# Layer 0's S5 tables and scan on VectorE, a gate's modulation on TensorE, and a reordered opening

## The chip, the cores and the metric

One core of a Trainium2 chip runs the whole program in one launch. The metric is the device time of an execution in microseconds; three runs of the kernel before gave a median of 1206.25 us.

## The reference

Two layers of a hybrid backbone work on 256 context tokens and 256 latent tokens of width 1024. Cut to what matters here (per layer, `p` its weights):

```python
sh1, sc1, ga1, sh2, sc2, ga2 = split(silu(c) @ w_mod[l] + b_mod[l], 6)     # and the same with c_ctx
h = rms_norm(x, g_norm1) * (1 + sc1) + sh1
z = h @ w_in[l]                    # 5 blocks of 256 for the mixers, then 4 gates of 1024
s5: bu = B_bar u;  states = associative_scan(a, bu) forward and backward (complex, 16 groups x 64)
    y = C_re h_re - C_im h_im + d * u;  y = gelu(y);  y = y * sigmoid(y @ w_glu)
fnet: real(fft2(u)) @ w;  pool: centred means of 2, 4, 8, 16, minus u
conv: v * sigmoid(gate), 31 taps, layer norm, silu, @ w
x = x + ga1 * (sum_k sigmoid(gate_k) * (branch_k @ w_branch_k)) @ w_out
x = x + ga2 * (relu(h2 @ w1) ** 2) @ w2          # h2: modulated with sh2, sc2
```

The context passes through layer 0 in full and through layer 1 only as far as the S5 states, which the latent scans inherit. Before the first layer a positional embedding is added to the latent tokens; behind the last stands an RMS norm.

## The kernel before

All tokens lie transposed: 128 features on the partitions, 512 token columns (context 0 to 255, latent 256 to 511) free, `X` in eight such tiles. Each large product is done on TensorE as three fp32r matmuls of a split operand (`mm3`): weight tiles arrive by DMA into three raw buffers, ScalarE copies the high part (`Stream.high`), VectorE subtracts to get the remainder (`Stream.low`, 1024 elements), and a tile of 128 outputs takes 24 matmuls (`tile_mm`). Both kinds of parts are in the tile "parts". The weight stream's DMAs go on SP's queue in the order of `plan`.

The order of instructions on each engine is the order of emission, which a planner makes in Python. TensorE's large products are emitted in a fixed order (`layer`, `order`). Between them, `pump` steps through background generators (`start(gen, classes, rank)`): the lowest rank that is ready goes first, provided that the modelled clock of each engine in its classes is at most a lead (2 us for VectorE and ScalarE, 5 for GpSimd) ahead of TensorE's modelled clock. A generator's `yield "w", t` makes it ready t modelled us later. Each engine executes its own list in order and waits on semaphores. The modelled clocks come from `Engines`: a cost per instruction, without waits between engines. `finish` emits all of a task that is left, and stands ahead of each branch's use (`y` in the order string: pool, FNet, convolution, S5).

The S5 branch of layer 0 needs tables from its parameters. `prep` makes the discretised `bbar` and the powers `base` on VectorE (some thirty short stretches of 16-element operations), and `rev`, the powers reversed, with nine copies on GpSimd. `tables_b` makes eight units: six products and sums of 256 elements each on VectorE, four TensorE transposes, a ScalarE copy and a store to DRAM (`scr_b`). `tables_c` makes eight units likewise on GpSimd (classes "pa"), with small matmuls and stores to `scr_c` and `scr_k`, its C loaded in pieces on SP's queue. In layer 0 both have two buffers (`nb = 2`), and the products of a unit are emitted after the next unit's elementwise work. Then `S5L.run` loads tables and u back (`load_u`, on GpSimd's queue), `states` makes the local states on TensorE, and `scan` runs a three-level up-sweep, seven small steps and a three-level down-sweep: the forward direction on GpSimd, the backward one on VectorE, five operations per level each (`level`). `readout` follows. Both scan tiles and the convolution's buffers of layer 0 carry the tile name "scan". The convolution is 62 `scalar_tensor_tensor` steps of 512 elements on VectorE with rank 4. For layer 1 the same table functions run on GpSimd beside layer 0's MLP, in one buffer (`nb = 1`), with waits of 8.0 and 2.0 around each unit's products; the tile is named "tables".

Modulation: the first shift and scale of layer 0 (`w_mod`, sixteen parts of 512 KB) are made on TensorE in the opening (`mod_part`, eight matmuls each; `mod_finish`). All others, from the first gate `ga1` (tiles 16 to 23) on, are made by `mods` on VectorE: per tile of 128 outputs a load (`w_modt`) and two accumulating operations of 1024 elements, rank 7.5, started after FNet's branch is used.

The opening (`run`, and the first branch of `layer`): x, modulation and first weight tiles are loaded; the position is added on VectorE and, for tiles 1, 3 and 5, on GpSimd; ScalarE squares; VectorE adds the eight squares up; TensorE sums over partitions; the norm's chain follows (`norm_steps`), then `h_tiles` makes the split input tile by tile, while `group(k, j)` emits the three matmuls of contraction tile k for output tile j and `parts` the modulation parts. `warm` emits matmuls whose result is not used.

## Time and profile before

| | before |
|---|---|
| three runs, us | 1206.25 median, 1205.58 to 1209.96 |
| the profiled execution, us | 1209.18 |
| its span, first to last instruction, us | 1207.2 |
| mean granted TensorE clock | 0.986 |
| TensorE, VectorE, ScalarE, GpSimd busy, us | 1160.9, 976.1, 517.1, 282.9 |

PE is TensorE's matmuls, PEld its weight loads, DVE VectorE, ACT ScalarE, POOL GpSimd, SP the queue of SyncE. Nearly all instructions carry the line of one helper (L64), so tiles tell them apart. Matmul rows of fp32 count two per instruction. An engine's idle time costs nothing unless another waits for it; the granted clock is given as a share of 2.4 GHz. Each fall of the clock in this trace lasts 3.4 or 6.8 us at 0.5.

### The profile page before, as it was taken

How to read it: one execution, taken by the hardware profiler on the slowest of the kernel's cores; microseconds unless marked ns; L12 is line 12 of the kernel's file. 1: busy time of each engine (PE TensorE's matmuls, PEld its weight loads, DVE VectorE, ACT ScalarE, POOL GpSimd, SP SyncE). 2: the span in 40 equal slices, each digit the busy share in tenths (PEclk: the TensorE clock that was granted, in tenths of full speed). 3: DMA queues.
4: the chain of work that ended last, by engine and by line, in shares of the span. 5: the costliest groups of instructions: out<-in, count | busy, mean ns of one | idle time of the engine just before them, and what ended most of it. 6: DMA issues, size and time to landing. Idle time of an engine off the chain costs nothing.

```text
span 1207.2 us, 20297 instructions
## 1 busy us (share of the span) xinstructions
PE 1160.9 (96%) x7770; PEld 1009.4 (84%) x7770; DVE 976.1 (81%) x1878; ACT 517.1 (43%) x872; POOL 282.9 (23%) x319
## 2 busy tenths in 40 slices
PE   7999897999999999999999899999899999999997
PEld 5777675777888988888887778898899999999997
DVE  6789989977999769999988883546998788867764
ACT  4534242344324365422332333346544556645543
POOL 0038656000000100166555561020520001000000
PEclk9999999999999999999999999999899999999999
DMA  9543531644674514466578774425554545555551
GB/s 366 225 144 109 180 92 52 229 156 138 212 229 156 173 37 148 140 188 230 186 245 296 249 247 180 130 98 177 173 166 167 159 160 205 177 190 179 189 182 48
DMA packets 66513, 211.49 MB, mean 175 GB/s; under 512 B 7984, under 2 KB 13616, under 8 KB 66416
## 3 DMA queue, kind: packets, MB, share of 16 engines
q1 hardware_dynamic: 55456, 183.84, 45.4%
q10 hardware_dynamic: 7696, 14.56, 3.3%
q0 software_dynamic: 3264, 11.80, 2.9%
q8 instruction: 61, 1.00, 0.3%
q14 instruction: 36, 0.29, 0.1%
HBM read 199.19 MB, written 10.98 MB: 174 GB/s over the span
## 4 chain that ended last, share of the span: by engine, by line
PE 72%; DVE 15%; POOL 3%; DMA 3%; issue 3%; ACT 3%; ACTq 0%; POOLq 0%; DVEq 0%; SPq 0%
PE bank L64 72%; DVE scan L64 5%; DVE parts L64 4%; DVE mixer L64 2%; DVE whole L64 2%; ACT parts L64 2%; POOL tables L64 1%; POOL whole L64 1%; ACT whole L64 1%; DVE windows L64 1%; POOL scan L64 1%; DMA whole<-in_w_in_dram 1%; DMA whole<-in_x_dram 0%; DMA scan<-scr_z 0%; DMA scr_c<-tables 0%
## 5 line engine op out<-in xcount | busy, mean ns | idle before, releaser
L64 PE MATMUL bank<-parts 128*128 128x512 f32 (+2 forms) x4008 | 727.2, 339 | 19.0 <-DVE parts L64 16.6
L64 PEld LDWEIGHTS bank<-parts 128*128 128x128 f32 x4008 | 616.3, 191 | 105.4 <-DVE parts L64 22.3
L64 ACT ACTIVATE parts<-whole 128x1024 fp32r<-128x1024 f32 (+1 forms) x288 | 273.7, 959 | 144.9 <-PE bank L64 73.9
L64 DVE TENSOR_TENSOR parts<-whole,parts 128x1024 fp32r<-128x1024 f32 (+1 forms) x240 | 294.0, 1233 | 16.0 <-ACT parts L64 15.6
L64 PE MATMUL bank<-hidden,parts 128*128 128x256 f32 (+1 forms) x1440 | 251.2, 335 | 0.0
L64 PEld LDWEIGHTS bank<-hidden,parts 128*128 128x128 f32 x1440 | 217.5, 188 | 29.9 <-issue 0.3
L64 DVE SCALAR_TENSOR_TENSOR whole<-whole 128x1024 f32<-128x1024 f32 (+4 forms) x188 | 175.7, 936 | 15.2 <-DMA whole<-in_w_modt_dram 12.0
L64 POOL TENSOR_TENSOR whole<-whole 128x256 f32<-128x256 f32 (+1 forms) x69 | 50.3, 743 | 347.2 <-ACT whole L64 342.2
L64 DVE SCALAR_TENSOR_TENSOR whole<-bank,whole 128x256 f32<-128x256 f32 (+1 forms) x121 | 54.7, 475 | 66.4 <-PE bank L64 66.2
L64 ACT ACTIVATE whole<-whole 128x256 f32<-128x256 f32 (+2 forms) x139 | 48.9, 388 | 107.2 <-DVE whole L64 96.4
L64 ACT ACTIVATE mixer<-bank 128x512 f32<-128x512 f32 (+1 forms) x84 | 40.7, 496 | 119.8 <-PE bank L64 110.3
L64 DVE TENSOR_TENSOR whole<-whole 128x256 f32<-128x256 f32 (+7 forms) x158 | 73.0, 467 | 16.7 <-ACT whole L64 11.7
L64 ACT ACTIVATE whole<-bank 128x512 f32<-128x512 f32 (+2 forms) x69 | 35.5, 537 | 109.1 <-PE bank L64 77.5
L64 POOL TENSOR_TENSOR tables<-tables,whole 128x256 f32<-128x256 f32 x48 | 61.4, 1287 | 37.4 <-DMA scr_c<-tables 34.9
L64 DVE TENSOR_TENSOR hidden<-whole,hidden 128x512 fp32r<-128x512 f32 (+2 forms) x77 | 53.4, 698 | 9.0 <-ACT hidden L64 2.4
L64 ACT ACTIVATE hidden<-whole 128x512 fp32r<-128x512 f32 (+2 forms) x77 | 47.1, 615 | 8.2 <-PE bank L64 2.3
L64 ACT ACTIVATE tables<-bank 128x512 f32<-128x512 f32 (+2 forms) x20 | 8.4, 422 | 92.8 <-PE bank L64 92.5
L64 POOL COPY whole<-whole 128x32 f32<-128x32 f32 x20 | 11.9, 626 | 150.3 <-DVE whole L64 150.3
L64 POOL TENSOR_TENSOR scan<-scan,whole 128x256 f32<-128x256 f32 (+3 forms) x50 | 44.0, 892 | 12.0 <-DVE scan L64 8.3
L64 DVE SCALAR_TENSOR_TENSOR scan<-scan,whole 128x512 f32<-128x512 f32 (+1 forms) x64 | 42.7, 728 | 0.0
L64 PE MATMUL bank<-merged,parts 128*128 128x256 f32 (+1 forms) x240 | 38.0, 316 | 0.8 <-DVE merged L64 0.8
L64 DVE TENSOR_TENSOR scan<-scan,whole 128x256 f32<-128x256 f32 (+5 forms) x61 | 31.5, 543 | 9.0 <-ACT whole L64 8.0
(115 smaller groups left out, 899.0 us busy)
## 6 DMA issues: line engine op xcount, KB each, us to landing
whole<-in_w_dram SPq DMA_DIRECT2D x128, 512.0 KB, 4.3
whole<-in_w_in_dram SPq DMA_DIRECT2D x84, 512.0 KB, 4.3
whole<-in_w_modt_dram SPq DMA_DIRECT2D x78, 512.0 KB, 4.1
whole<-in_w_br_dram SPq DMA_DIRECT2D x16, 512.0 KB, 4.4
whole<-in_w_out_dram SPq DMA_DIRECT2D x16, 512.0 KB, 4.2
mixer<-in_w_mod_dram SPq DMA_DIRECT2D x8, 512.0 KB, 9.7
scan<-scr_b POOLq DMA_DIRECT2D x8, 512.0 KB, 5.2
scan<-in_w_mod_dram SPq DMA_DIRECT2D x6, 512.0 KB, 9.7
```

The lines of the kernel that those rows point to most:

```text
L64: return f(out, *a, **k)
```

## The change

- Cost model: 0.14 + 1.055e-3 per element on VectorE; an fp32r matmul of n columns counts n + 32 in place of n; lags 2.75 and 1.71 in place of 2.5 and 1.52.
- Two kinds of background wait are new: `"u", e, t` (ready t after the later of TensorE's and engine e's modelled clocks) and `"at", t` (ready at a modelled time). They replace fixed waits in the tables of layer 0, pool, convolution and S5's end.
- `tables_b` and `tables_c` (both layers): five small ScalarE copies lay out the operands, and `turned` does a unit in three operations of 512 elements. Layer 0's `tables_c` and `scan_tables` run on VectorE; layer 1's stay on GpSimd, with one C buffer instead of two and 2.0 more wait after every second unit. ScalarE negates C.
- Scan (both layers): the backward direction's states are stored reversed (by ScalarE), so that one operation of up to 1024 elements does both directions, all on VectorE, four per level. `readout` reverses them back with two ScalarE copies per group.
- Modulation tiles 16 to 23 are made by `mods_pe` on TensorE (eight parts, from a new layout `w_modg`), a task that starts with the convolution and is finished ahead of FNet's use; `mods` starts at tile 24.
- Opening: position in one load at the head of ScalarE's queue, the parameters of S5 ahead of x on SP's queue; three early warm-up matmuls instead of seven; all position adds on VectorE; squares are added in pairs and TensorE sums each pair into one bank (`self.sums`); `prep` steps, parts and groups are interleaved more finely; ten modulation loads ahead of the norm instead of eight.

```diff
-                n = (n if a[1].dtype == F32R else 4 * max(n, 96)) * min(1.0, out.shape[0] / 128)
+                n = n + 32 if a[1].dtype == F32R else 4 * max(n, 112) * min(1.0, out.shape[0] / 128)
...
+    def turned(self, E, out, x, y, P, space):
+        sh, t = [128, 4, 16, 8], self.K.tmp()
+        w = []
+        for i, p in enumerate(P):
+            w.append(space[:, 32 * i:32 * i + 32])
+            self.K.nc.scalar.activation(w[i].rearrange("p (r q s) -> p r q s", r=2, q=2),
+                                        bc(p[:, None], [128, 2, 2, 8]), AF.Copy)
...
+        E.tensor_tensor(ov, bc(x[:, :, :, None], sh), wv[0], op=MUL)
+        E.tensor_tensor(tv, bc(y[:, :, :, None], sh), wv[1], op=MUL)
+        E.tensor_tensor(out, out, t, op=ADD)
...
     def tables_b(self, A, E):
-            E.tensor_tensor(ba[:, 0], Bb[0], Pb[0], op=MUL)
-            E.tensor_tensor(tmp, Bb[1], Pb[1], op=MUL)
-            E.tensor_tensor(ba[:, 0], ba[:, 0], tmp, op=SUB)
-            E.tensor_tensor(ba[:, 1], Bb[0], Pb[1], op=MUL)
-            E.tensor_tensor(tmp, Bb[1], Pb[0], op=MUL)
-            E.tensor_tensor(ba[:, 1], ba[:, 1], tmp, op=ADD)
+            nc.scalar.activation(x, bb[:, :, k, qs], AF.Copy)
+            nc.scalar.activation(y[:, 0], bb[:, 1, k, qs], AF.Copy, scale=-1.0)
+            nc.scalar.activation(y[:, 1], bb[:, 0, k, qs], AF.Copy)
+            self.turned(E, BAs[i % nb], ..., P, space[:, 128:192])
             yield
             if nb == 1:
                 yield "w", 8.0
+            done.append(nc.clock["d"])
             if i >= nb - 1:
+                yield "at", done[i + 1 - nb] + 0.5
                 products(i + 1 - nb)
...
+    def level(self, i, p0, step, n, g0=0):
+        x, cur = at(p0 - 2 ** i), at(p0)
+        E.tensor_tensor(t1, x, w(self.WR[i]), op=MUL)
+        E.tensor_tensor(t2, x[:, ::-1], w(self.WI[i]), op=MUL)
+        yield
         E.tensor_tensor(cur, cur, t1, op=ADD)
-        E.tensor_tensor(t2[:, h:2 * h], at(p0 - d, 0, 16), w(self.WI[i][k], 16, 32), op=MUL)
         E.tensor_tensor(cur, cur, t2, op=ADD)
...
+    def mods_pe(self):
+        for g in range(2):
+            for kp in range(4):
+                nc.sync.dma_start(raw, self.I["w_modg"][g][kp])
+                yield "w", 7.0
+                for k in range(2):
+                    for j in range(4):
+                        nc.tensor.matmul(bank[32 * j:32 * j + 32, 0:128], self.CACT[:, 2 * kp + k, :], w[:, k, j],
+                                         start=kp == 0 and k == 0, stop=kp == 3 and k == 1, tile_position=(0, 32 * j))
+                yield "w", 1.0
...
     def run(self):
-            self.tab0.append(self.start(self.pre[0].tables_c(half[1], nc.gpsimd), "pa", 2.5))
+            self.tab0.append(self.start(self.pre[0].tables_c(half[1], nc.vector), "da", 2.5))
             self.tab0.append(self.start(self.pre[0].tables_b(half[0], nc.vector), "d", 3.5))
...
-            (nc.gpsimd if k in (1, 3, 5) else nc.vector).tensor_tensor(x, x, pe, op=ADD)
+            nc.vector.tensor_tensor(x, x, pe, op=ADD)
...
+            if k % 2:
+                nc.vector.tensor_tensor(sq[k - 1], sq[k - 1], sq[k], op=ADD)
+                for i in range(4):
+                    nc.tensor.matmul(self.sums[:, i:i + 1], sq[k - 1][:, 128 * i:128 * i + 128], self.ones[:, 0:1],
+                                     start=k == 1 and i == 0, stop=k == 7 and i == 3)
+                if k < 5:
+                    self.warm(1)
```

## Rows read from the trace of the kernel before

**Rows 1.** page, part 1: busy time, share of the span, instructions

```profile
PE 1160.9 (96%) x7770; PEld 1009.4 (84%) x7770; DVE 976.1 (81%) x1878; ACT 517.1 (43%) x872; POOL 282.9 (23%) x319
```

**Rows 2.** windows by stage: stretch, length, busy PE PEld DVE ACT POOL, PEclk, DMA, GB/s

```profile
22.50:54.50 32.00, 30.84 (x293) 22.74 (x294) 22.85 (x70) 17.06 (x30) 0.00 (x0) 1.00 0.65 260
76.00:215.00 139.00, 123.32 (x722) 96.04 (x721) 130.54 (x223) 48.85 (x122) 94.05 (x114) 0.94 0.33 110
215.00:420.00 205.00, 205.00 (x1248) 167.22 (x1247) 176.85 (x292) 76.58 (x107) 6.10 (x7) 1.00 0.56 187
640.00:740.00 100.00, 95.79 (x502) 75.87 (x502) 78.38 (x109) 35.50 (x81) 55.92 (x63) 0.98 0.75 257
855.00:920.00 65.00, 60.33 (x580) 57.77 (x580) 63.84 (x149) 28.66 (x46) 23.85 (x31) 0.95 0.44 147
```

**Rows 3.** waits of PE, 76 to 215 us: total us, times, longest

```profile
PE bank L64 <- DVE parts L64: 7.8, 1, 7.8
PE bank L64 <- POOL scan L64: 3.9, 2, 2.1
PE bank L64 <- DMA scan<-scr_z: 2.2, 1, 2.2
PE bank L64 <- DVE scan L64: 1.6, 2, 1.0
```

**Rows 4.** busy us in a short stretch at the largest wait, columns as in rows 2

```profile
208.00:216.00 8.00, 4.58 (x12) 3.64 (x13) 7.96 (x11) 1.06 (x1) 3.01 (x4) 0.57 0.40 143
```

**Rows 5.** groups by form, 76 to 215 us: busy us, mean ns | idle before

```profile
L64 DVE TENSOR_TENSOR scan<-whole 128x256 f32<-128x256 f32 x16 | 12.5, 782 | 0.0
L64 DVE TENSOR_TENSOR scan<-scan 128x512 f32<-128x512 f32 x4 | 6.0, 1495 | 0.1
L64 DVE SCALAR_TENSOR_TENSOR scan<-scan,whole 128x512 f32<-128x512 f32 x44 | 29.7, 740 | 0.0
L64 POOL TENSOR_TENSOR scan<-scan,whole 128x256 f32<-128x256 f32 x38 | 32.9, 875 | 1.9 <-DMA scr_c<-scan 0.4
L64 POOL TENSOR_TENSOR scan<-scan,whole 128x512 f32<-128x512 f32 x2 | 6.2, 3120 | 1.8 <-issue 1.7
L64 ACT ACTIVATE scan<-whole 64x64 f32<-64x64 f32 x16 | 4.1, 255 | 5.3 <-POOL scan L64 5.1
```

**Rows 6.** groups by form on DVE, 1000 to 1180 us, GpSimd silent

```profile
L64 DVE TENSOR_TENSOR hidden<-whole,hidden 128x256 fp32r<-128x256 f32 x32 | 13.6, 425 | 3.3
```

**Rows 7.** groups by form on DVE, 340 to 420 us

```profile
L64 DVE SCALAR_TENSOR_TENSOR whole<-whole 128x1024 f32<-128x1024 f32 x9 | 11.0, 1223 | 0.2
L64 DVE TENSOR_TENSOR mixer<-mixer 128x512 f32<-128x512 f32 x9 | 6.2, 691 | 0.3
```

**Rows 8.** timeline of the opening: start us, us, engine, operation, count

```profile
4.47 6.32 PE L64 MATMUL bank<-whole 128*128 128x256 f32 x14 [4.47 <-DMA whole<-in_x_dram]
13.38 3.26 PE L64 MATMUL bank<-whole 128*128 128x256 f32 x16
15.71 0.16 DVE L64 TENSOR_SCALAR whole<-bank 128x4 f32<-128x4 f32 x1 [1.15 <-PE bank L64]
20.68 0.68 DVE L64 TENSOR_TENSOR whole<-whole,bank 128x512 f32<-128x512 f32 x1
```

**Rows 9.** groups by form on PE, 0 to 55 us: modulation parts

```profile
L64 PE MATMUL bank<-mixer,whole 128*32 128x128 f32 x128 | 4.7, 276 | 0.5 <-DMA mixer<-in_w_mod_dram 0.5
```

**Rows 10.** the tile scr_c, 76 to 215 us: its DMAs

```profile
DMA to landing us min/median/max: 2.0/2.1/5.1
```

**Rows 11.** waits of PE, 640 to 740 us

```profile
PE bank L64 <- POOL tables L64: 4.2, 3, 3.0
```

**Rows 12.** groups by form on POOL, 500 to 740 us

```profile
L64 POOL TENSOR_TENSOR tables<-tables,whole 128x256 f32<-128x256 f32 x48 | 61.4, 1287 | 37.4 <-DMA scr_c<-tables 34.9
```

**Rows 13.** waits of PE, 855 to 920 us

```profile
PE bank L64 <- DVE parts L64: 4.6, 2, 3.2
```

More of the change, by code (lines that the diff above doesn't have):

```diff
@@ L273, in tables_b @@
         nb = 2 if l == 0 else 1
-        BAs, BATs = [A(512) for _ in range(nb)], [A(512) for _ in range(nb)]
+        BAs, BATs, spaces = [[A(w) for _ in range(nb)] for w in (512, 512, 192)]
         def products(i):
@@ L324, in load @@
         def load(u):
-            (nc.gpsimd if l else nc.sync).dma_start(CCs[u % 2], K.I["s5c"][l][u])
-        load(0)
-        load(1)
+            (nc.gpsimd if l else nc.sync).dma_start(CCs[u % nb], K.I["s5c"][l][u])
+        for u in range(nb):
+            load(u)
         yield "w", 2.6
@@ L571, in scan @@
[L571 to L582 removed]
+        self.ST = [T(1024), T(1024)]
@@ new lines, in scan @@
+        S = self.SB.rearrange("p (a g n) -> p a g n", a=32, g=2)
+        E.memset(S[:, :, 0, 0:1], 0.0)
+        C3 = C.rearrange("p (a n) -> p a n", n=9)
+        Cr = C.rearrange("p (r a n) -> p r a n", r=2, n=9)
+        E.memset(C3[:, :, 0:1], 0.0)
+        for i, p0, step, n in ((0, 1, 2, 16), (1, 3, 4, 8), (2, 7, 8, 4)):
+            yield from self.level(i, p0, step, n)
+        C4 = C3[:, :, 1:9].rearrange("p a (g n) -> p a g n", g=2)
+        E.tensor_copy(C4, S[:, :, :, 8:33:8])
+        t1, t2 = [t[:, 0:32].rearrange("p (r a) -> p r a", r=2) for t in self.ST]
@@ L629, in readout @@
                 yield from K.hold(2)
+                back = K.tmp()[:, 0:256].rearrange("p (r q n) -> p r q n", r=2, q=4)
+                for r in range(2):
+                    nc.scalar.activation(back[:, r], SB[:, r, 1, 4 * h:4 * h + 4, g, 0:32][:, :, ::-1], AF.Copy)
+                yield "u", "a", 0.5
+                yield from K.hold(2)
                 py = [K.aux(), K.aux()]
@@ L925, in said @@
                 task["cls"] = y[1]
+            elif y[0] == "u":
+                c = self.nc.clock
+                task["ready"] = max(c["t"], c[y[1]]) + y[2]
+            elif y[0] == "at":
+                task["ready"] = y[1]
             else:
@@ L1059, in mods @@
                 yield
-        for i in range(16, 96):
+        for i in range(24, 96):
             l, m = i // 48, i % 48
@@ L1309, in weight @@
                 gw.append(self.stream.take(("in", l, gm[j])))
+            prep = tab[0]
             parts(2)
-            self.warm(2)
-            norm = self.norm_steps(((self.ACC,),), 512, 1024)
+            norm = self.norm_steps((), 512, 1024, pss=[self.sums])
             next(norm)
@@ L1346, in layer @@
             next(h)
-            group(1, 1)
+            self.step(prep, 1)
+            group(2, 0, 1)
+            parts(1)
+            weight(2)
+            group(3, 0, 1)
+            parts(1)
+            self.step(prep, 3)
             group(0, 2)
             group(1, 2)
-            self.step(tab[0], 3)
-            group(2, 0, 1, 2)
             parts(1)
+            group(2, 2)
             weight(3)
-            group(3, 0)
             parts(1)
-            group(3, 1)
-            parts(1)
-            parts(1)
-            group(3, 2)
             self.mod_finish(4)
@@ L1438, in layer @@
         tconv = self.start(br.conv(), "d", 4.0)
+        if l == 0:
+            tgate = self.start(self.mods_pe(), "a", 3.2)
         tasks = {2: task, 3: tconv}
@@ L1697, in make0 @@
             yield from self.pre[0].prep(half[1])
-            self.tab0.append(self.start(self.pre[0].tables_c(half[1], nc.gpsimd), "pa", 2.5))
+            self.tab0.append(self.start(self.pre[0].tables_c(half[1], nc.vector), "da", 2.5))
             self.tab0.append(self.start(self.pre[0].tables_b(half[0], nc.vector), "d", 3.5))
         self.tab0.append(self.start(make0(), "d", 0.0))
-        self.mod_load()
-        while self.stream.load():
-            pass
-        self.step(self.tab0[0], 1)
-        self.mod_ahead = 8
+        prep = self.tab0[0]
+        self.step(prep, 1)
+        for k in range(0, 8, 2):
+            nc.sync.dma_start(self.X[:, k:k + 2, :], I["x"][:, k:k + 2, :])
+        for ahead in (3, 4, 8):
+            self.mod_ahead = ahead
+            self.mod_load()
+            self.stream.load()
+            if ahead == 4:
+                self.step(prep, 1)
+        self.mod_ahead = 10
         self.mod_load()
         nc.vector.memset(self.CACT, 0.0)
-        self.warm(7)
+        self.step(prep, 2)
         t = self.tmp()
```

284 lines of the change are left out of this document (137 added, 147 removed).

## The prediction

> **What bounds the kernel now.** I read the page's busy shares first, then busy time and granted clock by stage, then what TensorE waited for in the stages where it was not full, and then what the other engines' instructions cost there. TensorE is busy for 96% of the span, VectorE for 81%, GpSimd for 23% [rows 1]. So the gain of any edit is limited to the places where TensorE does not run, or runs at its lower clock. By stage [rows 2] TensorE is full at clock 1.00 from 215 to 420 us: nothing that this change does to VectorE can shorten that. The poor stages are 76 to 215 us (layer 0's mixer while its S5 tables and scan are made: TensorE 123.3 of 139 us, clock 0.94, VectorE 130.5, GpSimd 94.1), 640 to 740 us (layer 1's tables: clock 0.98) and 855 to 920 us (layer 1's scan: clock 0.95).
>
> In the first of these TensorE waits 15.5 us: 7.8 for one weight remainder (parts) that stands on VectorE behind the scan, 3.9 for table products on GpSimd, 2.2 for the stored u (scr_z), whose load stands on GpSimd's queue behind its small table operations, 1.6 for table products on VectorE [rows 3]. The clock of 0.94 takes another 0.06 x 139 = 8.3 us; every fall stands behind one of these waits. In the last one TensorE works only 4.6 of 8 us while the clock is 0.57 [rows 4]; I take 1.4 us of the loss as lying inside the wait, so 6.9. Together 22.4 us are to be had here.
>
> Why VectorE and GpSimd run late shows in the durations. While both work, a VectorE product of 256 elements takes 0.78 us, GpSimd's 0.88, and the scan's VectorE additions of 512 take 1.50 [rows 5]; with GpSimd silent a 256 product takes 0.43 [rows 6], and 512 take 0.69 [rows 7]. The emitter's cost model (0.12 + 1.04e-3 per element) prices them as alone, so it issues work on which TensorE then waits.
>
> The Trainium skill (SBUF — State Buffer, "SBUF: two separate sides") says that VectorE with two SBUF inputs and GpSimd take one port pair by an exclusive lock, so that the loser waits for the other's whole instruction. 0.43 becoming 0.78 agrees. By the rule the convolution's operations, which read two SBUF inputs too, should also be shortened by the change; their row says 0.740 us beside GpSimd [rows 5], which leaves little to gain, and I count nothing for them.
>
> **The change part by part.**
>
> *Tables and scan of layer 0.* Before, 48 products of 256 on VectorE (at 0.78: 37 us) and 48 on GpSimd (at 0.88: 42 us); after, 16 units of three operations of 512 on VectorE, 48 x 0.69 = 33 us, none on GpSimd. The merged scan has six levels of four operations; by 0.69 for 512 elements, 1.22 for 1024 [rows 7] and 0.43 for 256 it is 8 x (1.22 + 0.69 + 0.43) = 18.7 us on VectorE, where before both engines shared it at 1.50 and 3.12 for one 512 operation [rows 5]. So VectorE's load stays near 130 us, and what exceeds the stage is the convolution's 44 steps (rank 4, at 0.74), which may slide into 215 to 420 us, where VectorE has 205 - 176.9 = 28 us free [rows 2]. The cross-engine order goes (no GpSimd result is waited for, u's load is free at once), and the model's costs (0.14 + 1.055e-3: 0.68 for 512) become what the rows show. All 15.5 + 6.9 could go.
>
> What is late next: each unit on VectorE waits for five small ScalarE copies (0.255 us each [rows 5]: 1.3 us); a CA buffer is used again two units later, after its store has landed (2.1 us median, 5.1 at most [rows 10]); and ScalarE negates C itself, hence waits for that load. VectorE is in order, so its weight remainders stand behind such a wait. Bounds: 0, when the two-deep buffers cover it, and 16 x 1.3 = 21 us, when every copy group is waited for in full and TensorE with it. The products come one unit late, which covers most; I take 4 us.
>
> *First gate's modulation on TensorE.* 16 accumulations of 1.22 us [rows 7] (19.5 us) leave VectorE in a stretch where TensorE does not wait for it: nothing gained. TensorE gets eight parts, now in a full stage: 128 rows, which are eight parts, took 4.7 us [rows 9]. Bounds 0 (they fall into gaps) and 4.7 plus a late load; I take 4.7. So the stage is -22.4 + 4 + 4.7 = -13.7 us.
>
> *Opening.* The norm's chain begins at 15.7 us and the first layer-0 tile input at 20.7 [rows 8]. Before, the last square is followed by up to five adds of 0.69 in a row; after, by one, as TensorE sums pairs. That is 2 to 2.8 us, less what the three position adds that come from GpSimd cost (3 x 0.43 = 1.3, partly while x arrives). From 22.5 to 54.5 us TensorE is busy 30.8 of 32 us [rows 2], so spreading the groups finds about 1 us. Against this, the table preparation's steps, its two loads (one now ahead of x on SP's queue) and the steps' small operations are moved into this stretch on VectorE. Bounds -6 and +3; I take -2.5.
>
> *Layer 1's tables stay on GpSimd*, with three operations of 512 for six of 256. TensorE waited 4.2 us for them [rows 11], with 0.02 x 100 = 2 us of clock [rows 2]. A unit was 6 x 1.29 = 7.7 us of work after a wait for the store of 34.9 / 7 = 5.0 us [rows 12]: 12.7 us, and the slot must be about 12.5, since three of sixteen were late. The waits in modelled time become 6% shorter in real time (a matmul of 512 columns counted 512, now 544): a slot of 11.9. No row shows a GpSimd product of 512 beside this work: at least 1.29 (a 256 one), at most 3.12 [rows 5]. I take 1.29 + 0.88 = 2.1, one more 256's length on top: 3 x 2.1 + 5.0 = 11.3, on time. I take -3 of the 6.2 us.
>
> *Layer 1's scan* goes to VectorE whole. VectorE is full there (63.8 of 65 us), TensorE waits 4.6 us for weight remainders [rows 13] and loses 0.05 x 65 = 3.3 to the clock [rows 2]. The work that comes over costs about what the slowing took; but two ScalarE permutations ahead of the wait are not touched. Bounds 0 and -7.9; I take -4. The remaining waits ("u" and "at" for fixed ones, longer lags) sit on tasks that run beside full TensorE stages: 0, within 3 either way.
>
> Sum: -2.5 - 13.7 - 3 - 4 = -23.2 us. The profiled execution took 1209.18 us (span 1207.2 and 2.0 around it), so 1186.0; it was 2.9 above the median of the runs, 1206.25, on which scale the forecast is 1183 us.
>
> **Rivals.**
>
> *The waits come back in another form* (half the gain): VectorE stands behind ScalarE's copies and the stores, so that of layer 0's stage 12 us more stay, and opening and layer 1's scan give 3 less: 1183 + 15 = 1198. For it: VectorE has only 8 us free in the stage and every weight remainder passes it. Against: TensorE's largest wait is one event behind contended operations.
>
> *A cold opening.* The early warm-up matmuls fall from seven to three. At the start fourteen rows of 256 columns took 6.32 us, 0.45 each, which is the lower level, 1.2 GHz; later sixteen rows, half of them sums of one column, took 3.26 [rows 8]. If the rise comes only with the dense groups, parts, warm-ups and the first groups double: some 6 us more, partly while data is awaited: opening +3, total 1189. The Trainium skill (TensorE: Matmul & The Clock Gate, "What's actually happening") holds that the throttled state is the default and activity releases it, which speaks for this rival; the rise in the trace after the unbroken warm-ups agrees.
>
> *The other side: layer 1's tables on GpSimd become the bound.* If an operation of 512 takes 3.12 us there, as one did in the scan, a unit of tables_c is 3 x 3.12 + 5.0 = 14.4 against 11.9, 2.5 us late eight times, and one of tables_b, which starts 2.0 + 1.3 us after the last products, 12.7, 0.8 late: 26 us, and after each of the eight long waits a clock fall of 1.7 us, as after the one long wait now: 40 us. With the other gains of 20 it gives 1206 + 20 = 1226. It decides from 2.6 us per operation on (8 x 0.9 + 13.6 = 21). For it: the rows of 3.12. Against: VectorE gives up 20 us of gate work, so the two meet less.
>
> *The change does less than it says:* layer 0's preparation keeps its nine reversed copies on GpSimd, just ahead of the tables; they can contend for some 4 us, which is in the 4 us kept above.
>
> **How the numbers follow.** 0.5% (6 us) is about what can be told from no change. Forecast 0.60, its own range 1175 to 1193; half the gain 0.18, half of which reaches above 1200; cold opening 0.12; other side 0.08; nearly all of it gained (opening -6, nothing late) 0.02, at 1172. The range 1173 to 1204 leaves out the other side and the tails. Faster: 0.60 + 0.12 + 0.02 + 0.09 = 0.83; within 0.5%: 0.09; slower 0.08.
>
> **What would show it.** In the profile after: GpSimd's busy time in 76 to 215 us near zero; VectorE's 512 operations at 0.69; no TensorE wait on GpSimd's scan tile and none of several us on a remainder; clock 1.00 through the stage. Right or wrong for the parts: the norm at 13 to 14 us; eight more parts in layer 0's mixer; layer 1's 512 products between 1.3 and 2.6 us. The prediction is wrong if TensorE waits over 10 us in layer 0's mixer, if VectorE shows idle time behind ScalarE or stores there, or if layer 1's table waits exceed 5 us.

## The result, and the profile after

The changed kernel takes 1224.38 us (median, 1221.04 to 1232.16), the kernel before 1208.11 on the same chip: a ratio of 1.0149, 95% interval 1.0111 to 1.0187. The forecast was 1183; the change makes the kernel slower by 16 us. The profiled execution took 1232.16 us, the slowest of its four, 23.0 more than that of before.

First the busy shares of the changed kernel, which answer to [rows 1]: GpSimd has lost 152 us, VectorE 23, ScalarE has gained 23, and TensorE's share has fallen.

```profile
PE 1172.9 (95%) x7910; PEld 1012.9 (82%) x7910; DVE 952.7 (77%) x1818; ACT 540.2 (44%) x1032; POOL 130.6 (11%) x134
```

Then its windows by stage, columns as in [rows 2].

```profile
22.50:54.50 32.00, 26.47 (x233) 16.77 (x230) 19.61 (x56) 14.02 (x25) 0.00 (x0) 0.89 0.57 219
76.00:215.00 139.00, 135.96 (x908) 104.67 (x907) 109.66 (x215) 64.10 (x203) 9.22 (x14) 1.00 0.45 156
215.00:270.00 55.00, 55.00 (x387) 44.78 (x386) 54.83 (x74) 16.71 (x25) 2.54 (x4) 1.00 0.50 165
270.00:300.00 30.00, 22.17 (x143) 13.27 (x142) 14.59 (x34) 13.08 (x21) 0.72 (x1) 0.77 0.25 94
640.00:740.00 100.00, 92.89 (x482) 73.47 (x480) 84.63 (x113) 37.93 (x100) 35.56 (x26) 1.00 0.79 266
855.00:920.00 65.00, 59.39 (x550) 57.21 (x549) 59.05 (x124) 31.54 (x61) 4.06 (x6) 1.00 0.53 180
```

The stage from 76 to 215 us did become what was forecast: TensorE 136 of 139 us at clock 1.00, GpSimd 9 us. Two other stretches became poor: 22.5 to 54.5 (clock 0.89) and 270 to 300, which lay within the full stage of [rows 2] and now has 22.2 of 30 us at 0.77.

A ruler for the rest: I counted TensorE's products with split operands in order of time (one of 512 columns as two) in both traces and compared the time at which the same count is reached; the lag is the time after less the time before. The order of these products is nearly the same in both kernels.

```
count   before   after    lag   what lies between
    0     22.5    27.8   +5.3   start, norm, first tile
  150     49.8    65.4  +15.6   the opening's groups
  450     83.8    99.5  +15.6
 1500    269.2   264.7   -4.5   layer 0's mixer
 1650    293.1   302.8   +9.7   the convolution's projection (y30)
 1950    327.1   342.2  +15.1   the state scan's readout and tail
 5100    709.6   722.2  +12.7   layer 1's tables
 5250    727.8   749.7  +22.0   their end
 6750    938.4   962.1  +23.7   layer 1's scan
```

The 20 us gained up to count 1500 are partly work not done yet: the convolution's tail and the scan's readout. At 1950 everything that the mixer's branches need is done in both (the state scan's projection, y00, follows at about count 2016), and the whole mixer has gained 0.5 us.

What TensorE waited for from 76 to 215 us in the changed kernel (compare [rows 3]; two more waits are of 0.2 us each), and from 270 to 300 us, where the kernel before waited for nothing:

```profile
PE bank L64 <- ACT whole L64: 1.4, 1, 1.4
PE bank L64 <- DMA whole<-in_w_modg_dram: 0.6, 1, 0.6
PE bank L64 <- ACT scan L64: 0.5, 1, 0.5
```

```profile
PE bank L64 <- DVE scan L64: 7.8, 3, 3.9
```

TensorE's timeline from 270 us shows the convolution's tail (sums, norm, linear) coming out step by step with little beside it, since the program finishes this task just ahead of its projection.

```profile
277.07 1.05 PE L64 MATMUL bank<-whole,scan 128*128 128x1 f32 x8 [0.74 <-DVE scan L64]
282.02 2.04 PE L64 MATMUL bank<-scan,whole 128*128 128x512 f32 x2 [3.90 <-DVE scan L64]
287.26 6.05 PE L64 MATMUL bank<-scan,whole 128*128 128x512 f32 x7 [3.20 <-DVE scan L64]
```

VectorE's groups from 76 to 215 us (compare [rows 5]): each operation costs what was forecast, but the engine stands idle ahead of them.

```profile
L64 DVE SCALAR_TENSOR_TENSOR scan<-scan,whole 128x512 f32<-128x512 f32 x23 | 15.6, 742 | 0.0
L64 DVE TENSOR_TENSOR scan<-scan 128x512 f32<-128x512 f32 x18 | 13.2, 732 | 15.2 <-ACT scan L64 15.1
L64 DVE TENSOR_TENSOR whole<-scan 128x512 f32<-128x512 f32 x16 | 10.9, 684 | 0.0
```

Its waits from 72 to 280 us (total, times, longest) add up to 28.4 us behind ScalarE, most of them while convolution steps were left to run; only 23 of those steps fell ahead of 215 us, 44 before [rows 5].

```profile
DVE scan L64 <- ACT scan L64: 17.3, 9, 4.5
DVE parts L64 <- ACT parts L64: 8.2, 1, 8.2
DVE scan L64 <- ACT whole L64: 2.9, 1, 2.9
```

In the opening (compare [rows 8]) the norm starts at 17.74 us, not 15.71, and the first tile at 25.94, not 20.68. Its lines on TensorE and VectorE:

```profile
5.43 2.93 PE L64 MATMUL bank<-whole 128*128 128x256 f32 x6 [5.43 <-DMA whole<-in_x_dram]
11.73 1.71 PE L64 MATMUL bank<-whole,mixer 128*128 128x1 f32 x8
18.49 1.08 PE L64 MATMUL bank<-mixer,whole 128*32 128x128 f32 x16
27.81 0.50 PE L64 MATMUL bank<-parts 128*128 128x512 f32 x1 [1.04 <-ACT parts L64]
29.47 0.74 PE L64 MATMUL bank<-parts 128*128 128x512 f32 x2 [1.16 <-DVE parts L64]
```

```profile
14.28 0.69 DVE L64 TENSOR_TENSOR whole<-whole 128x512 f32<-128x512 f32 x1 [0.88 <-ACT whole L64]
17.74 0.16 DVE L64 TENSOR_SCALAR whole<-bank 128x4 f32<-128x4 f32 x1 [2.26 <-PE bank L64]
25.94 0.69 DVE L64 TENSOR_TENSOR whole<-whole,bank 128x512 f32<-128x512 f32 x1 [0.63 <-PE bank L64]
```

GpSimd's table operations of layer 1 (compare [rows 12]): 82 us for 48 of 512 elements, 5.1 us a unit, and the engine idles for ScalarE's copies now.

```profile
L64 POOL TENSOR_TENSOR tables<-tables,whole 128x512 f32<-128x512 f32 x16 | 32.2, 2011 | 1.3
L64 POOL TENSOR_TENSOR whole<-tables 128x512 f32<-128x512 f32 x16 | 27.4, 1711 | 1.0 <-DVE whole L64 1.0
L64 POOL TENSOR_TENSOR tables<-tables 128x512 f32<-128x512 f32 x16 | 22.4, 1399 | 120.0 <-ACT tables L64 80.9 <-DMA scr_c<-tables 30.5 <-ACT parts L64 8.5
```

### The profile page after: what moved, and what is told of

Read it like the earlier page. It is cut to its first block, busy times and chain, and to the rows that moved or that the text cites. A ratio compares the mean times of both kernels' runs of the same rounds, so it can differ in the third digit from the quotient of the medians.

```text
span 1230.4 us, 20471 instructions
## 1 busy us (share of the span) xinstructions
PE 1172.9 (95%) x7910; PEld 1012.9 (82%) x7910; DVE 952.7 (77%) x1818; ACT 540.2 (44%) x1032; POOL 130.6 (11%) x134
## 4 chain that ended last, share of the span: by engine, by line
PE 72%; DVE 13%; DMA 6%; issue 4%; ACT 3%; POOL 0%; ACTq 0%; SPq 0%; DVEq 0%; POOLq 0%
PE bank L64 72%; DVE whole L64 5%; DVE parts L64 4%; DMA whole<-in_w_modt_dram 3%; DVE mixer L64 2%; DVE scan L64 1%; ACT parts L64 1%; ACT whole L64 1%; DMA scr_c<-tables 1%; ACT scan L64 1%; DMA scan<-scr_b 1%; DVE windows L64 1%; DMA whole<-in_w_in_dram 1%; DMA scan<-in_s5c_dram 0%; DMA whole<-in_cc_dram 0%
## 5 line engine op out<-in xcount | busy, mean ns | idle before, releaser
L64 DVE SCALAR_TENSOR_TENSOR whole<-whole 128x1024 f32<-128x1024 f32 (+3 forms) x174 | 161.5, 929 | 14.6 <-DMA whole<-in_w_modt_dram 11.6
L64 ACT ACTIVATE whole<-whole 128x256 f32<-128x256 f32 (+3 forms) x117 | 47.0, 426 | 100.6 <-DVE whole L64 97.1
L64 DVE TENSOR_TENSOR whole<-whole 128x512 f32<-128x512 f32 (+6 forms) x154 | 63.1, 421 | 13.0 <-ACT whole L64 11.4
L64 POOL TENSOR_TENSOR whole<-whole 128x256 f32<-128x256 f32 (+1 forms) x38 | 23.0, 619 | 347.6 <-ACT whole L64 347.1
L64 DVE TENSOR_TENSOR scan<-scan 128x512 f32<-128x512 f32 (+4 forms) x65 | 31.5, 493 | 18.7 <-ACT scan L64 17.9
L64 PE MATMUL bank<-whole 128*32 128x128 f32 (+4 forms) x270 | 31.6, 315 | 8.7 <-DMA whole<-in_x_dram 5.4
L64 DVE TENSOR_TENSOR scan<-scan,whole 128x512 f32<-128x512 f32 (+3 forms) x48 | 29.8, 644 | 13.1 <-ACT whole L64 10.8
L64 DVE TENSOR_TENSOR mixer<-bank,mixer 128x512 f32<-128x512 f32 (+1 forms) x56 | 31.4, 569 | 9.0 <-PE bank L64 9.0
```

Of the source, the lines that this page charges most:

```text
L64: return f(out, *a, **k)
```

## The experiments

The ratios are to the kernel before, run on the same chip, with 95% intervals.

**The opening as a whole.** In o1 the functions that issue it are those of the kernel before, in the changed kernel; in o2 the reverse.

> The changed kernel with the opening of the kernel before (its loads' order, seven warm-ups, sums of squares folded on VectorE, its order of parts, weights and groups), all else as changed. In the traces the changed kernel stood 5.3 us behind at the first product of the first group (22.5 against 27.8 us) and 15.6 us behind at the 150th large matmul (49.8 against 65.4), and that lag stayed. Theory: the whole 15.6 us is the opening's own, so this kernel takes about 1224 - 15 = 1209 us. Rival: the new opening also carried 17 steps of the table preparation instead of 10, and the stage after it gained 20 us from that; then the preparation comes later here, the convolution is later still at its projection, and a third to a half of the 15 us is given back there: 1214 to 1217 us.

> The kernel before with the new opening alone (loads, three warm-ups, sums of squares' pairs added by TensorE, new order of groups, 17 preparation steps); tables, scan, first gate and waits stay as before. Theory (the opening's loss is its own): about 1208 + 15.6 = 1223 us. Rival: the stage after it, which idled 15.5 us at waits in the kernel before, takes part of the delay up, since its tables start with more of the preparation done: 1213 to 1217 us. By the forecast on record the opening alone was worth -2.5 us: 1205.5 us.

o1: 1218.97 us, 1.0088 (1.0060 to 1.0117). o2: 1219.08, 1.0081 (1.0053 to 1.0108). The ruler shows the opening undone or added in full (lag at count 150: +0.5 in o1, +15.3 in o2) and then a part lost or made up: +4.6 in o1 and +11.2 in o2 at count 1950. So the new opening costs 10 us in the kernel before, and its removal gives 5 us (by the medians) to 7 us (by the ratios) of the 16. o2 lies between theory and rival, nearer the rival; o1 lies beyond its rival (1214 to 1217): less came back than either allowed.

**Its parts.** o4 has the lines of the kernel before from the first parts to the last group (parts, weights, groups, warm-ups and three preparation steps fewer), with the new sums kept; o3 has more warm-ups, o5 earlier parts, o6 the old sums:

```
o3
-        self.warm(3)
+        self.warm(7)
-                if k < 5:
-                    self.warm(1)
+                if k < 7:
+                    self.warm(3)
o5
-            parts(2)
+                if k in (3, 5):
+                    self.mod_part()
o6
-                nc.vector.tensor_tensor(sq[k - 1], sq[k - 1], sq[k], op=ADD)
...
+            if k in (3, 4):
+                nc.vector.tensor_tensor(sq[k - 3], sq[k - 3], sq[k - 1], op=ADD)
...
-            norm = self.norm_steps((), 512, 1024, pss=[self.sums])
+            norm = self.norm_steps(((self.ACC,),), 512, 1024)
```

> The changed kernel with the old order of parts, weights, groups and warm-ups after the norm's start; kept are the new loads, three warm-ups, pairs of squares summed by TensorE and 14 preparation steps in the opening. The opening as a whole cost 10 to 15 us up to the first groups' end. Theory: most of it is the order, in which the next group needs the tile that is just being made (five waits of 0.8 to 1.7 us and four of 0.7 us on the chain parts, copy, product, VectorE, ScalarE, VectorE) and the low clock between them: the 150th product stands 8 to 11 us earlier than in the changed kernel. Rival: the cold start decides (three warm-ups, pair sums at half clock): the first group is as late as before, 27 us, the lag at the 150th product stays at 12 to 15 us, and the time at 1222 to 1225 us.

> The changed kernel with more warm-up matmuls ahead of the norm: seven instead of three before the sums, and three instead of one after each of the first three pair sums, nothing else. Theory A (cold start): the pair sums (1.71 us for eight rows) and the first parts run at the lower clock for want of work before them; with more of it the clock is up earlier, the norm starts 1 to 3 us earlier, and the lag of 5.3 us at the first group falls to 3 or less: 1219 to 1222 us. Theory B (the steps in front of the norm: sums on TensorE, preparation steps and additions all on VectorE): the lag stays at 5 us or grows by the warm-ups' own time: 1224 to 1227 us.

> The changed kernel with its first two modulation parts issued between the pair sums (one after the second pair's warm-up, one after the third pair's sums) instead of behind the last pair's. Theory: TensorE's queue is in order, and the four parts that the first layer-0 tile needs stand behind the sums, so that two fewer of them (2.1 us at the lower clock, 1.3 at the higher) and what follows come 1.5 to 2.5 us earlier: first group at 25.5 to 26.5 us instead of 27.8. Rival: the chain of additions and squares (2.24 us a pair) and the norm's steps on VectorE set it: first group stays at 27 to 28 us. In the time either is hard to see: 1221 to 1225 us.

> The changed kernel with the squares folded by VectorE's additions into one accumulator again, eight sum matmuls at the end instead of 32 in four portions; three warm-ups, new loads and the new order of groups stay. Theory (TensorE's queue from the first matmul to the fourth part is itself the path: the pair sums take 7.1 us of it in the changed kernel's trace and the parts stand behind them): the first group starts at 23 to 25 us instead of 27.8, and since the new order keeps its own 10 us the lag at the 150th product falls from 15.6 to about 12: 1220 to 1223 us. Rival (the additions on VectorE and the three position additions that came over from GpSimd): first group at 27 to 28 us, 1224 us.

o4: 1231.63 us, 1.0175 (1.0135 to 1.0216). The first group is as late (+5.9) but the lag is still +5.9 at count 150: the new order costs 10 us, as expected. The time does not show it: the lag has grown to +24.3 by count 1950. From 76 to 300 us TensorE waits 12.1 us for VectorE's scan tile and 7.6 for the gate's weights there; the preparation is three steps behind the changed kernel's, but what of the growth comes from that was not tried.

A scale for the next three: c1, c2, c3, t1, p1 and l1 below have the changed kernel's opening line by line, and their first groups start at 25.9 to 27.9 us, their lags at 150 lie between +12.6 and +15.7. o3: 1223.02, 1.0140 (1.0099 to 1.0181), between its two theories. The clock is up by the pair sums (eight rows in 0.95 us, not 1.71), yet the first group comes at 26.8 us and the lag at 150 is 14.5, both within that scatter: no gain is shown. o5: 1225.25, 1.0123 (1.0085 to 1.0160), first group at 28.1. o6: 1225.64, 1.0141 (1.0103 to 1.0180), first group at 28.1, with the granted clock at 0.65 from 10 to 22.5 us. The copy that ends the first four parts stands at 23.2 to 24.5 us in all of these, at 17.7 in the kernel before and 18.3 in o1. No single one of these edits removes the 5 us of the first group; which combination would, stays open. What the lower clock costs in such a place, k1 and k4 below show: they have the old opening, but the clock stood at 0.50 from 13.3 to 20.1 and from 14.5 to 21.3 us, and their first groups start at 25.6 and 26.4 us, where k2 and k3, with the same lines up to there, have 22.4 and 23.0.

**Scan, convolution and tables.** c1 and c2 change one rank each; t1 lets the table task give way between ScalarE's copies and VectorE's products; c3 is c2 with t1; p1 puts the C tables back on GpSimd.

```
c1
-        tconv = self.start(br.conv(), "d", 4.0)
+        tconv = self.start(br.conv(), "d", 4.0 if l else 2.0)
c2
-                    tasks[0] = self.start(s5.run(), "a", 0.0)
+                    tasks[0] = self.start(s5.run(), "a", 4.5)
t1 (in turned, behind the copies)
+        if self.l == 0:
+            yield "u", "a", 0.3
+        t = self.K.tmp()
p1
-            self.tab0.append(self.start(self.pre[0].tables_c(half[1], nc.vector), "da", 2.5))
+            self.tab0.append(self.start(self.pre[0].old_tables_c(half[1], nc.gpsimd), "pa", 2.5))
```

> The changed kernel with one number changed: the rank of layer 0's convolution, 2.0 instead of 4.0, so that its steps go ahead of both table tasks (2.5 and 3.5) wherever VectorE is free. Theory: the 19.6 us lost at the convolution's projection (270 to 293 us) come from the convolution being last in rank while the tables, now on VectorE too, fill it; with the rank raised that wait goes and the tables still end before the scan is needed: about 1224 - 18 = 1206 us. Rival 1: VectorE as a whole is short of time there (waits at ScalarE's copies included), so the wait only moves to the state scan's projection: 1218 to 1226 us. Rival 2: the wait is the serial tail of the convolution (its norm and its linear), which stays: 1214 us.

> The changed kernel with a pause put between ScalarE's copies of a table unit and VectorE's three 512-element operations on them (layer 0 only): the task gives way until ScalarE's clock has passed, so that steps of the convolution stand in front of the operations instead of behind them. Theory: VectorE's idle time at ScalarE's copies between 72 and 280 us (17.3 + 8.2 us in the trace) is filled with convolution steps, which then end some 10 to 17 us earlier: about 1224 - 12 = 1212 us. Rival 1: rank alone decides (the convolution is still behind the tables, which now take longer by the pauses): 1222 to 1228 us. Rival 2: that idle time stood outside the chain that ends at the projection: 1224 us.

> The changed kernel with one number changed: layer 0's state-scan task starts with rank 4.5 instead of 0.0, so that the convolution (4.0) goes ahead of the scan, but still behind the tables. In the trace with the copies ahead, the convolution's 60 steps ended at 213.6 us, its sums' matmuls ran at 223.2 us, and the rest of it then stood still until 269 us while VectorE ran the scan, which is now on VectorE alone and outranks it; its tail came out at the projection all the same. Theory: the wait at the convolution's projection (some 10 us without products and 10 us at the lower clock) is the scan standing in front of the convolution on VectorE; here it goes, and the scan and its readout still end before the projection that needs them: 1224 - 14 = 1210 us (1206 to 1215). Rival 1: VectorE's time is short over the whole mixer, so the wait goes over to the state scan's projection: 1222 to 1245 us (as the convolution put ahead of the tables did, 1247). Rival 2: the tail itself is the wait, whatever stands in front: 1224 us.

> The rank of the scan behind the convolution (4.5) together with the pause between ScalarE's copies and the table products. Theory (two causes in a row: the copies hold up the convolution's steps, the scan holds up its tail): the pause alone gave nothing because the scan stood behind it; with both, the convolution ends 20 to 30 us earlier and the scan starts no later than with the rank alone: 1205 us (1200 to 1210), some 5 us below the rank alone. Rival 1 (VectorE's total decides): like the rank alone, within 3 us. Rival 2: the pauses end the tables later, and with the scan last the wait at its projection grows: 1220 to 1235 us.

> The changed kernel with layer 0's C tables in the form and on the engine of the kernel before (48 operations of 256 elements on GpSimd), all else as changed. Theory: the change moved work onto VectorE, which then has too much to do up to the convolution's projection; taken off it again (24 operations of 0.69 us, and some waits at ScalarE's copies), the convolution ends earlier and the wait there shrinks by about as much, less what GpSimd's work adds to VectorE's own small operations (782 against 425 ns in the kernel before): 1224 - 8 = 1216 us. Rival 1 (the two engines hold each other up, as the change assumes): 1224 us or more. Rival 2: the scan's rank alone decides, and it only starts earlier: 1222 to 1226 us.

c1: 1247.45 us, 1.0321 (1.0269 to 1.0374), beyond all that was expected: the wait at y30 goes, but the tables end later and TensorE waits 22 us between 215 and 400 us, 10.5 of them in one wait for ScalarE's copies of the scan. t1: 1226.14, 1.0136 (1.0096 to 1.0176): nothing gained, and its trace says why. VectorE's timeline: the last convolution steps, the scan's first level, the scan's last level, and only then the convolution's tail.

```profile
210.32 3.40 DVE L64 SCALAR_TENSOR_TENSOR scan<-scan,whole 128x512 f32<-128x512 f32 x5
222.66 2.36 DVE L64 TENSOR_TENSOR scan<-scan,whole 128x1024 f32<-128x1024 f32 x2 [7.71 <-ACT scan L64]
264.85 2.48 DVE L64 TENSOR_TENSOR scan<-scan 128x1024 f32<-128x1024 f32 x2
268.98 1.28 DVE L64 SCALAR_TENSOR_TENSOR scan<-bank,scan 128x512 f32<-128x512 f32 x2
```

The convolution's steps were done at 213.7 us, but its tail waited until 269: the scan now runs on VectorE alone and has the highest rank. This led to c2: 1219.40, 1.0077 (1.0053 to 1.0100), and with both c3: 1214.28, 1.0045 (1.0027 to 1.0064). In both the wait at y30 is gone (270 to 300 us is full at clock 1.00 in c2) and a smaller one appears at y00, lag from -3.0 to +4.6 between counts 1950 and 2100 in c3. Each gained 9 us less than expected. VectorE's load up to y00 is the next limit: in k4 below, which has 24 products fewer on VectorE than k2, the lag stays at +0.4 between these counts, where k2's grows by 7.6. TensorE's waits from 270 to 350 us in c2:

```profile
PE bank L64 <- DVE scan L64: 4.7, 1, 4.7
PE bank L64 <- issue: 1.7, 1, 1.7
```

p1: 1216.97, 1.0067 (1.0041 to 1.0093), as expected. With 24 products off VectorE nothing waits from 215 to 300 us; instead TensorE waits for GpSimd again from 76 to 215:

```profile
PE bank L64 <- POOL scan L64: 7.0, 4, 2.8
PE bank L64 <- DMA whole<-in_w_modg_dram: 1.7, 1, 1.7
```

**The first gate.** g1 has all modulation rows on VectorE.

```
-        self.mod_tile = 24
+        self.mod_tile = 16
-            tgate = self.start(self.mods_pe(), "a", 3.2)
```

> The changed kernel with the first gate's modulation back among VectorE's products (all 80 modulation rows there, none on TensorE). Theory: TensorE's eight parts cost 4.7 us and hold one accumulator bank for most of 60 us; without them the mixer stage is 4 to 6 us shorter, and VectorE's sixteen extra products fall after the mixer, where it has room: 1224 - 5 = 1219 us. Rival 1: the bank held is what delays the state scan's readout (it needs two banks free): 10 us or more gained, 1212 us. Rival 2: the products that come back to VectorE are needed before the output projection and arrive late: 1228 to 1235 us.

g1: 1248.86 us, 1.0309 (1.0277 to 1.0341), 19 us (by the ratios) to 24 us (by the medians) slower than the changed kernel. The eight parts on TensorE save far more than their 5 us. That VectorE has no room for these rows in time (rival 2, and more than it said) is argued: no trace at the full clock shows where it waits.

**Layer 1's tables.** l1 has the two table functions of the kernel before for layer 1.

```
-                        yield from self.pre[1].tables_b(self.APRE, E)
-                        yield from self.pre[1].tables_c(self.APRE, E)
+                        yield from self.pre[1].old_tables_b(self.APRE, E)
+                        yield from self.pre[1].old_tables_c(self.APRE, E)
```

> The changed kernel with layer 1's tables in the form of the kernel before (six operations of 256 elements a unit on GpSimd, two buffers for the C rows, the old waits), all else as changed. Theory: the last C unit waited for its store and TensorE for it (6.97 us at 736 us, within 11 us of such waits), because the single buffers put loads, copies and stores in a row; with the old form that end wait goes: 1224 - 6 = 1218 us. Rival: the new form does take less of GpSimd, and the wait at 736 us is one execution's: in the traces of the changed kernel with the old opening or the copies ahead it is not there: 1223 to 1228 us.

l1: 1234.30 us, 1.0209 (1.0178 to 1.0240), slower than the changed kernel by 7 (by the ratios) to 10 us (by the medians). The theory fell: the new form is the better one here. The ratios' intervals just touch (1.0178 and 1.0187), the executions do not, and l1's lag grows from +14.2 at count 3900 to +27.3 at 4950, where the changed kernel's falls. TensorE waited for the old form, from 600 to 740 us:

```profile
PE bank L64 <- POOL tables L64: 11.0, 5, 3.1
```

**A mended version.** k1 has the old opening, c2's rank and t1's pause; k2 also more preparation steps at the old opening's three places; k3 is k2 with the scan's rank 0.0; k4 is k2 with p1's tables.

```
-            self.step(tab[0], 3)
+            self.step(tab[0], 5)
```

> The changed kernel with the old opening, the scan's rank behind the convolution (4.5) and the pause between ScalarE's copies and the table products: the three places undone or mended, the rest of the change kept (tables and scan on VectorE, first gate on TensorE, layer 1's tables and scan). Theory (three separate losses): the two ranks' kernel with the new opening took 1214 us and stood 15.7 us behind the kernel before at the 150th product, then gained; with the old opening it saves what the old opening saved alone and a part is given back since seven preparation steps come later: 1214 - 8 = 1206 us (1201 to 1209), faster than before or the same. Rival (VectorE's total up to the state scan's projection is the bound, so an earlier start is given back there): 1210 to 1215 us.

> The same as the kernel with all three, and six more preparation steps within the old opening (five at each of its three places instead of three), which idled VectorE 12 of the 54 us from 22 to 76. Theory: the preparation's late steps are what the old opening gives back, so the tables and with them the scan come some 4 to 6 us earlier: 1201 us (1197 to 1206), about 4 below. Rival 1: the steps stand in front of the first layer's tiles on VectorE and the opening is longer by as much: no gain, within 2 us of the kernel without them. Rival 2: the convolution and scan don't depend on the preparation's end: same within 2 us.

> The best kernel so far (old opening with six more preparation steps, pause after ScalarE's copies, scan behind the convolution) with the scan's rank back at 0.0, in front of the convolution. Theory: the scan's steps outrank the convolution's tail again, which comes out at its projection with 9 to 20 us of waits and low clock; a part of that is saved at the state scan's own projection, where the other kernel waits: 1201 + 6 = 1207 us (1204 to 1212). Rival (with everything earlier there is room for both): 1201 us, within 2.

> The best kernel so far with layer 0's C tables on GpSimd again, in the form of the kernel before. Theory (in the mended schedule VectorE has room for them, and GpSimd's work brings back TensorE's waits for its products, 8 us of them between 89 and 130 us in the run with these tables on GpSimd): slower, 1201 + 5 = 1206 us (1203 to 1210). Rival (VectorE's load is the bound up to the state scan's projection, where 8 to 10 us are still lost): faster, 1194 to 1198 us.

k1: 1208.57 us, 0.9996 (0.9976 to 1.0016). k2: 1201.09, 0.9939 (0.9914 to 0.9964), as expected, and faster than both kernels. k3: 1214.78, 1.0079 (1.0054 to 1.0104), more than expected. k4: 1204.13, 0.9965 (0.9940 to 0.9990), which can't be told from k2. Six preparation steps in a stretch where VectorE idled are worth 7 us (the two traces differ by more, since k1's has the low clock named above and a late store in layer 1), and the scan's rank 14 (by the medians) to 17 us (by the ratios). In k2 the stages of [rows 2] and the stretch of y30 are these:

```profile
22.50:54.50 32.00, 30.88 (x294) 22.78 (x295) 24.97 (x88) 17.03 (x31) 0.00 (x0) 1.00 0.65 257
76.00:215.00 139.00, 135.87 (x902) 104.57 (x901) 111.33 (x175) 61.50 (x200) 5.32 (x7) 0.99 0.49 165
215.00:300.00 85.00, 85.00 (x514) 67.92 (x513) 79.77 (x148) 32.12 (x48) 1.42 (x2) 1.00 0.46 148
```

k3 has TensorE's wait at y30 back (215 to 300 us):

```profile
PE bank L64 <- DVE scan L64: 9.4, 3, 4.1
```

## Why the prediction was wrong

Term by term, forecast and then ruler: opening -2.5 and +15.6 us, layer 0's mixer -13.7 and -0.5, layer 1's tables -3 and +6.9, layer 1's scan -4 and +1.7. All three signs of being wrong came: TensorE waits 10.8 us between 76 and 345 us and 10.5 us for layer 1's tables, and VectorE stands idle behind ScalarE for 28.4.

*The stage (-22.4 us): right where it was made, false as a gain.* Waits fell from 15.5 to 2.9 us and the clock rose to 1.00, so 19.5 of the 22.4 us went. The step that failed is the next one, "the convolution's 44 steps (rank 4, at 0.74), which may slide into 215 to 420 us". They may not: y30 needs the convolution at about 270 us. I read 28 us of free VectorE from the stage's mean and did not ask by when the deferred work is due. From 270 to 300 us, 7.8 us of waits came back and 0.23 x 30 = 6.9 us of clock, of which 3.0 lie inside the waits (TensorE is busy for only 7.7 us of the low clock), so 3.9. With the eight parts at 5.2 us (forecast 4.7) the mixer's balance is -19.5 + 7.8 + 3.9 + 5.2 = -2.6, by the ruler -0.5; the other 2 us are not traced. c2, c3 and k3 show that the scan in front of the convolution makes this wait; t1 alone, that filling the idle time does not help while the scan stands there. The gate's rows were put at "nothing gained" for VectorE; in the changed kernel that is wrong by some 20 us (g1).

*New waits behind ScalarE (+4 us, bounds 0 to 21).* They were 20.2 us at the copies, near the upper bound, and 8.2 more at a weight's high part, but on VectorE; TensorE did not wait for them in the stage, and t1, which has 8.3 us for the 17.3 at the copies and 2.6 for the 8.2 at the high part, is no faster. An in-order engine's wait must be priced by the work behind it.

*The opening (-2.5 us, bounds -6 to +3): it cost 15.6.* Two steps failed. The first is that the last square is followed "by one" addition, "as TensorE sums pairs", for a gain of 2 to 2.8 us: each pair's addition now waits 0.88 us for a square just issued, and the squares behind it 1.09 us for the next position addition on VectorE:

```profile
13.10 1.15 ACT L64 ACTIVATE whole<-whole 128x512 f32<-128x512 f32 x2 [1.09 <-DVE whole L64]
```

So the last square ends at 14.25 us and its addition at 14.97 (14.28 + 0.69). In the kernel before they end at 11.90 and 14.57:

```profile
10.11 1.79 ACT L64 ACTIVATE whole<-whole 128x512 f32<-128x512 f32 x3
11.68 0.64 PE L64 MATMUL bank<-whole 128*32 128x128 f32 x16 [0.89 <-DMA whole<-in_w_mod_dram]
13.08 1.49 DVE L64 TENSOR_TENSOR whole<-whole 128x512 f32<-128x512 f32 x2
```

Behind it the pair's sums, at the lower clock, add 1.6 us up to the norm, and 3.2 more arise from the norm to the first tile, where sixteen rows of a part take 1.08 us until 22.6 us; in the kernel before they take 0.64 from 11.7 us on. The second is the new group order, which I priced at "about 1 us" of gain. It puts each group directly behind the parts, the modulation step, VectorE and ScalarE that make its tile; TensorE's clock was 0.89 from 22.5 to 54.5 us, and it waited 7.4 us between 22 and 76:

```profile
PE bank L64 <- DVE parts L64: 3.2, 3, 1.4
PE bank L64 <- ACT parts L64: 2.6, 2, 1.6
PE bank L64 <- ACT whole L64: 1.6, 4, 0.4
```

o4 takes 10 us of lag away by the order. The rival of a cold opening had the sign right, at +3, and a low clock cost 3 us in k1 and k4, which could be most of the 5 us of the first group, but not the 10 us of the order. The Trainium skill (TensorE: Matmul & The Clock Gate, "What's actually happening") says that activity releases the throttled state; o3's rows agree (0.95 against 1.71 us), though with its added warm-ups the first group came no earlier than the scatter allows.

*Layer 1's tables (-3 us).* By the ruler -2.4 up to count 5100, as forecast, then one wait of 6.8 us at the last unit, behind a store. The step that failed is the store's wait of 5.0 us a unit: here GpSimd waited 16.5.

```profile
727.47 0.45 ACTq L64 DMA_DIRECT2D whole<-in_smw_dram  x1
728.09 0.33 ACTq L64 DMA_DIRECT2D scr_c<-tables  x1
739.93 1.07 POOL L64 TENSOR_TENSOR tables<-tables 128x512 f32<-128x512 f32 x1 [16.50 <-DMA scr_c<-tables]
743.42 1.36 PE L64 MATMUL bank<-tables 128*32 128x112 f32 x24 [6.80 <-POOL tables L64]
```

The store was issued on ScalarE's queue 0.6 us behind the second of two loads of 896 KB and landed 11.7 us later. In k1, with the same distance, it took 11.2 and TensorE waited 6.1; 2.1 us behind (o3) it took 9.6, 4.1 behind (t1) 6.8; in o1 it stands ahead of the loads and took 2.4. k2 has no such wait either (-2.6 in all). That the loads made it late is read from these traces, not tried by itself. An operation took 1.4 to 2.0 us, between the bounds. The rival on the other side named the right sign with the wrong mechanism: its point of 2.6 us was not reached, and that its 1226 us lies near the 1224 measured is chance.

*Layer 1's scan (-4 us): nothing gained.* The clock is 1.00 in the window, not 0.95, but the kernel is 22 us later there and a fall of 3.4 us follows at 920.9 us (before: 6.8 us). TensorE still waits for the same remainders [rows 13]:

```profile
PE bank L64 <- DVE parts L64: 5.6, 2, 3.2
```

By VectorE's timeline the remainder of the second stands at 918.1 us behind the scan's last level, now wholly on VectorE; the first, of 3.2 us, is as long as before, so the sharing with GpSimd did not make it.

The sum by the ruler is 15.6 - 0.5 + 6.9 + 1.7 = 23.7 us at count 6750, against 23.0 between the profiled executions; without the 6.8 us wait it is near the 16 us between the medians.

## What to carry to other kernels

Work taken off one engine joins another in-order queue: ask by when each task behind it is due, and set ranks and early starts again in the same change. A stage that looks faster may have deferred work; compare two traces at the same count of useful work, and trust the lag only where both have done everything. An order that fed each product from a value just being made cost 10 us here, more than the gaps it filled. A store issued right behind two large loads on its queue took 9 us longer to land than one issued ahead of them: look at what stands in front of it.

## What the runs showed of the hardware

The slowing between VectorE and GpSimd shows in one kernel with and without GpSimd's work: VectorE's 512-element products of the tables, from 76 to 135 us, in p1 and then in the changed kernel.

```profile
L64 DVE TENSOR_TENSOR whole<-scan 128x512 f32<-128x512 f32 x6 | 6.4, 1072 | 0.0
```

```profile
L64 DVE TENSOR_TENSOR whole<-scan 128x512 f32<-128x512 f32 x8 | 5.5, 684 | 0.0
```

The rule that the prediction weighed (the Trainium skill, SBUF — State Buffer, "SBUF: two separate sides") agrees with these rows, but not with the convolution's operations, which also read two SBUF operands: 740 ns beside GpSimd, 742 with it nearly silent. In the kernel before, 17 of the 44 [rows 5] ran beside a GpSimd operation for over half of their time and took 734 to 745 ns, the other 27 733 to 745. What sets these apart from the products no run here shows.
